# First operands joined in one array of 3 KB rows, and the S5 matrices within a chunk in four column tiles

## The chip, the cores and the metric

The kernel runs on one core of one Trainium2 chip. The metric is the device time of one execution, in microseconds (us). The core has five engines that run side by side, each through its own queue in order: TensorE (PE; its weight loads are shown as PEld), VectorE (DVE), ScalarE (ACT), GpSimd (POOL) and SyncE (SP). SP and POOL issue the DMAs here. Line numbers (L1004) are those of the kernel before.

## The reference

A trunk of four residual layers over 256 tokens of width 1024, in float32. Layer i uses mixer i mod 3: a gated linear recurrence (HGRN2), a matrix memory (mLSTM), a state space (S5), then HGRN2 again. Every layer ends in a SwiGLU FFN with 2816 hidden units:

```
for i in range(4):
    h = mixer[i % 3](x)
    x = layernorm(alpha * x + h)
    x = layernorm(alpha * x + (silu(x @ w_gate) * (x @ w_up)) @ w_down)
```

Two places matter. First, the HGRN2 mixer of layer 0 begins with `q, f, v, g = split(x @ w_in, 4)`. Second, the S5 mixer has 64 groups of 16 channels, each with 64 complex states and a diagonal transition A:

```
state[t] = A * state[t-1] + B u[t]        y[t] = Re(C state[t]) + d * u[t]
```

The kernel cuts the 256 tokens into 64 chunks of four. What a token gives to the outputs of its own chunk is a small matrix per group, with Re(C A^k B) for k = 0 to 3 in its blocks and d on its diagonal. These are the matrices "within a chunk". They depend on the weights alone.

## The kernel before

**Products in three parts.** Each float32 weight or activation is split into a rounded high part, made by an ACT copy (L123 for weights, L1215 for the first x^T), and a low rest, made by a DVE subtraction (L124, L1216). `mm3` then makes a product with three TensorE matmuls: high x high (L140), low x high (L141), high x low (L142). Inside the FFN, `ws_wide` does the same in two matmuls (L170, L173).

**Weights.** `plan` lists all weight tiles in the order of their use, 1 MB each ([128, 2048] floats). `stage_next` takes the next: a DMA on SP's queue (L109) into one of three stage buffers, then the two splits for each half of 1024 columns, into one of eight pairs of split buffers. `wstage` hands out the tile that is due and keeps the staging one tile ahead.

**Start.** `warm_up` runs ten matmuls on zeros (L75). Then `trunk` loads x^T in three pieces, of 2, 2 and 4 row blocks k (L1213), splits each, and stages the first weight tile after the first piece. The first two tiles of layer 0 (w_hg 0 and 1, the two halves over k of the first 512 columns of v) come in three and two pieces (`cuts`, L107). `hgrn` takes them in `block`: `as_part` goes over the two tiles' four halves, in each over the two row halves h of the tokens, and in each of those over two k. The first result is v (L453); then come four gate pairs (`gates`), queries and scores. The POOL queue loads the identity (L50), the head norm weight hnw (L435) and the score masks msk (L439). The identity is read first at L584, msk at L598.

**FFN with S5 preparation beside it.** The FFNs of layers 0 and 1 call `fill` between their parts; it emits some pieces of `s5_prepare`. For each quarter q of the groups these are: `products_b` and `products_bj` (B A^j, on DVE, into the padded tile bz), `products_c` (C A^k for k = 1 to 4 into cu, on DVE, and into the padded cz, on ACT), and then for e = 0, 1: two `turn` (four TensorE transposes each, L987) and one `within`. `within` is called eight times in all.

**`within`.** For each of four group pairs x it makes a block of 32 rows with 64 columns: 16 columns with C itself (L1002, from bc) and 48 with C A^1 to C A^3 (L1004, from cu), each as a sum over the real and the imaginary part. All four land in PSUM partitions 0 to 31, beside one another. One DVE operation masks all of them by the parity pattern par (L1008), the diagonal d is added (L1007, L1010), ACT copies the blocks shifted for the later tokens (L1012), and SP writes the result out (L1013). `temps` gives scratch tiles: two buffers of t0, one of t1.

Each engine's work is put in an order of its own by the framework, which moves instructions where their operands allow it; DMAs on one queue are issued in that order, and a wait of one holds those behind it.

Of the kernel before, what the change touches and what calls it, by code (L numbers as in the profile page):

```python
# [9 lines left out]
F32 = mybir.dt.float32  # L10
# [24 lines left out]
class Trunk:  # L35
    def __init__(self, ctx, tc, aps):
        self.ctx, self.tc, self.nc, self.a = ctx, tc, tc.nc, aps
        mk = lambda name, bufs, **kw: ctx.enter_context(tc.tile_pool(name=name, bufs=bufs, **kw))
        self.const = mk("const", 1)
        self.stage = mk("stage", 3)  # L40
        self.split = mk("split", 8)
        self.xp = mk("xp", 3)
        self.gbp = mk("gbp", 1)
        self.small = mk("small", 4)
        self.ps = mk("ps", 2, space=bass.MemoryType.PSUM)
        self.dram = mk("dram", 1, space=bass.MemoryType.DRAM)
        self.n = 0
        c = self.const
        self.ident = c.tile([P, P], F32, name="ident")
        self.nc.gpsimd.dma_start(self.ident, aps["c_ident"])  # L50
# [17 lines left out]
    def warm_up(self, pool):  # L68


        z = pool.tile([P, 512], BF16, name="warm")
        self.nc.vector.memset(z, 0.0)
        ps = self.bank("t")
        for _ in range(10):
            self.nc.tensor.matmul(ps, z[:, 0:P], z, start=True, stop=True)  # L75


# [20 lines left out]
    def stage_next(self):  # L98

        nc = self.nc  # L100
        name, *at = self.plan[self.staged]
        src = self.a[name]
        for i in at:
            src = src[i]
        st = self.stage.tile([P, 2048], F32, tag="w", name=self.uid("w"))
        w = src.shape[-1]
        cuts = {0: (0, 512, 1024, w), 1: (0, 1024, w)}.get(self.staged, (0, w))  # L107
        for c in zip(cuts, cuts[1:]):
            nc.sync.dma_start(st[:, slice(*c)], src[:, slice(*c)])  # L109
        out = []  # L110
        for i in range(w // 1024):
            part = st[:, i * 1024 : (i + 1) * 1024]
            hi = self.split.tile([P, 1024], F32R, tag="hi", name=self.uid("hi"))
            lo = self.split.tile([P, 1024], F32R, tag="lo", name=self.uid("lo"))
            if name == "w_mo":
                for j in range(2):
                    k = 4 * (at[0] // 2) + 2 * i + j
                    r, c = self.rows[:, k : k + 1], slice(j * 512, (j + 1) * 512)
                    nc.scalar.activation(hi[:, c], part[:, c], AF.Copy, scale=r)
                    nc.vector.scalar_tensor_tensor(lo[:, c], part[:, c], r, hi[:, c].bitcast(F32), ALU.mult, ALU.subtract)  # L120
            else:
                for c in (slice(0, 1024),) if self.staged or i else (slice(0, 512), slice(512, 1024)):
                    nc.scalar.copy(hi[:, c], part[:, c])  # L123
                    nc.vector.tensor_tensor(lo[:, c], part[:, c], hi[:, c].bitcast(F32), ALU.subtract)  # L124
            out.append((hi, lo))
        self.ready[self.plan[self.staged]] = out
        self.staged += 1

    def wstage(self, *key, ahead=AHEAD):

# [300 lines left out]
    def hgrn(self, j, gb, lb=None):  # L431

        nc, tc = self.nc, self.tc
        nw = self.const.tile([P, 1], F32, name=f"hnw{j}")
        nc.gpsimd.dma_start(nw, self.a["hg_nw"][j])  # L435
        with tc.tile_pool(name=self.uid("hg"), bufs=1, reuse_waits="tile") as hp, \
                tc.tile_pool(name=self.uid("hw"), bufs=2, reuse_waits="tile") as wp:
            msk = hp.tile([P, len(MASKED), 256], F32, name=self.uid("msk"))
            nc.gpsimd.dma_start(msk, self.a["c_lvl"])  # L439
            ot = self.transposed(hp)  # L440
            v = hp.tile([P, 2, D], F32, name=self.uid("v"))
            g = hp.tile([P, 2, D], F32, name=self.uid("g"))
# [70 lines left out]
            def gates(pr):  # L513
                pre[pr] = self.hgrn_gates(wp, pr, pair_proj(8 + pr), lb)
# [12 lines left out]
            self.table("natural_log_exp_and_others")  # L527
            for pr in range(4):
                gates(pr)
            self.table("silu_and_others")  # L530
            query(0)
            query(1)
# [273 lines left out]
    def s5_prepare(self):  # L806
# [160 lines left out]

        def products_c(q):
            f = slice(8 * q, 8 * q + 8)
            cu, t1 = temps(2, 4, 8, 16)  # L970
            k["cu"] = cu
            for i in range(2):
                p = lambda r: pw[:, r, 0:4, f][:, :, :, None].broadcast_to([P, 4, 8, 16])
                x = k["bc"][:, 2 + i : 3 + i].broadcast_to([P, 4, 8, 16])
                tt(cu[:, i], x, p(0), ALU.mult)
# [19 lines left out]
        def within(q, e):  # L995
            b = 2 * q + e
            ps = self.bank("t")
            for x in range(4):
                f, o = 4 * e + x, ps[0:32, x * 64 : (x + 1) * 64]
                w = lambda i: k["bz"][:, i, f, 3].rearrange("p g c -> p (g c)")  # L1000
                for i in range(2):
                    nc.tensor.matmul(o[:, 0:16], w(i), k["bc"][:, 2 + i, f], start=i == 0, stop=i == 1)  # L1002
                for i in range(2):
                    nc.tensor.matmul(o[:, 16:64].rearrange("p (k c) -> p k c", k=3), w(i), k["cu"][:, i, 0:3, f], start=i == 0, stop=i == 1)  # L1004
            tm = k["tm"]
            dg = tile_("dg", [32, 4, 32])
            tt(dg, self.ident[0:32, None, 0:32].broadcast_to([32, 4, 32]), dd[:, 4 * b : 4 * b + 4, None].broadcast_to([32, 4, 32]), ALU.mult)  # L1007
            tt(tm[0:32].rearrange("p f (k g c) -> p (f k) g c", g=2, c=16), ps[0:32, 0:256].rearrange("p (n c) -> p n c", c=16)[:, :, None].broadcast_to([32, 16, 2, 16]),  # L1008
               par[:, None].broadcast_to([32, 16, 2, 16]), ALU.mult)
# [193 lines left out]
def trunk(tc, aps, out, layers=range(DEPTH), ffn=True):  # L1203
    with ExitStack() as ctx:
# [2 lines left out]
        layers = list(layers)  # L1207
        t.plan = plan(layers, ffn)
        with tc.tile_pool(name="first", bufs=1, reuse_waits="tile") as fp:
            src = fp.tile([P, KD, S], F32, name="xt")  # L1210
            t.warm_up(fp)
            for k in (slice(0, 2), slice(2, 4), slice(4, KD)):
                nc.sync.dma_start(src[:, k], aps["xt"][:, k])  # L1213
                y, dh, dl = src[:, k], t.xh[:, k], t.xl[:, k]
                nc.scalar.copy(dh, y)  # L1215
                nc.vector.tensor_tensor(dl, y, dh.bitcast(F32), ALU.subtract)  # L1216
                if t.staged == 0:
                    t.stage_next()
        spans = None
        late = ctx.enter_context(ExitStack())  # L1220
        for i in layers:
# [49 lines left out]
def consts():  # L1271
    s, c = np.arange(P)[:, None], np.arange(64)[None, :]
    lvl = []
    for m in MASKED:
# [3 lines left out]
    t = np.arange(P)[None, :]  # L1278
    return {
        "c_ident": np.eye(P, dtype=np.float32),  # L1280
        "c_par": np.repeat(np.eye(2, dtype=np.float32), 16, 0)[:, :, None].repeat(16, 2),
        "c_lvl": np.stack(lvl, 1).astype(np.float32),
        "c_caus": np.where(s > t, np.float32(BIG), np.float32(0.0)),
    }
# [2 lines left out]
def layout(i):  # L1287
# [2 lines left out]
    hg = []  # L1290
    for w in i["hgrn_w_in"]:
        hg.append(np.concatenate([cols_as(w[:, 2 * D : 3 * D]), cols_ws(w[:, 0 : 2 * D]), cols_as(w[:, 3 * D :])]))
    ml = i["mlstm_w_in"][0]
    gw = np.zeros((KD, P, P), np.float32)
    for g in range(2):
# [3 lines left out]
    gc = i["ffn_w_gate_up"].reshape(DEPTH, KD, P, 2, NBLK, 2, P).transpose(0, 4, 5, 2, 3, 1, 6).reshape(DEPTH, NBLK, 2, P, 2048)  # L1299
    out = {  # L1300
        "x": x,
        "xt": np.concatenate([x[:P], x[P:][::-1]]).T.reshape(KD, P, S).transpose(1, 0, 2),
        "ln": np.stack([i["ln_g"], i["ln_b"]], 2).reshape(2 * DEPTH, 2, D),
        "lb": i["hgrn_lb_logits"].reshape(DEPTH, HEADS, P).transpose(2, 0, 1),
        "w_hg": np.stack(hg),
# [37 lines left out]
```

## Time and profile before

| | |
|---|---|
| median of 3 runs | 1296.07 us (1295.36 to 1298.86) |
| the profiled execution | 1296.3 us |
| its span on the core | 1294.4 us |
| PE, PEld busy | 1273.3 us, 1073.3 us |
| DVE, ACT, POOL busy | 964.8 us, 710.5 us, 53.8 us |
| moved by DMA | 251.00 MB, mean 194 GB/s |

The span runs from the first to the last instruction of the core, and times within the trace count from its start. A row of the trace in order of time reads: start in us, length in us, engine, line, operation, what it writes <- what it reads, shape, how many; in brackets the idle time before it and what ended that. Busy times of TensorE overlap, since matmuls are pipelined: a matmul's length is longer than the distance to the next one's start. A float32 matmul that isn't split makes two records; a transpose makes one. In a table of windows the columns after the engines are the granted TensorE clock (1.00 is full), the share of the DMA engines' time, and GB/s.

### The profile page before, as it was taken

Reading aid. Unit: us, or ns where it says so; the run is one execution under the profiler, and the core shown is the slowest. Engines: PE = TensorE matmul, PEld = TensorE weight load, DVE = VectorE, ACT = ScalarE, POOL = GpSimd, SP = SyncE. Lnnn points to the kernel's source line nnn. Section 1 sums busy time; section 2 is a strip of 40 time slices with the busy share of each in tenths; the row PEclk is TensorE's granted clock in tenths of the full one; section 3 lists DMA queues with packets and bytes.
Section 4 is the critical chain, followed back from the end, with each engine's and each line's share of the span. In section 5 each row is a group of like instructions: output and inputs, shape, how many; then the busy total and the mean of one; then the engine's idle time right before and its main releaser. Section 6 shows DMA issues by size and latency. Waiting matters only on the chain.

```text
span 1294.4 us, 18807 instructions
## 1 busy us (share of the span) xinstructions
PE 1273.3 (98%) x7206; PEld 1073.3 (83%) x7206; DVE 964.8 (75%) x1664; ACT 710.5 (55%) x1134; POOL 53.8 (4%) x77
## 2 busy tenths in 40 slices
PE   8999999999999999999999999999999999999997
PEld 6987788888788888888878778888879878888885
DVE  5888789786688699768489887666595896766664
ACT  5755475665457555657442456555459544555550
POOL 0000200000100110000010000000010001000001
PEclk9999999999999999999999999999999999999999
DMA  8832376757374257756558737555555323755540
GB/s 313 298 131 100 126 247 213 253 179 261 123 260 163 98 202 254 241 199 230 193 219 292 269 131 260 195 184 180 190 208 187 134 97 116 265 190 192 181 149 32
DMA packets 46313, 251.00 MB, mean 194 GB/s; under 512 B 5344, under 2 KB 9456, under 8 KB 19856
## 3 DMA queue, kind: packets, MB, share of 16 engines
q1 hardware_dynamic: 45712, 248.08, 54.0%
q0 software_dynamic: 512, 1.73, 0.4%
q8 instruction: 56, 0.92, 0.3%
q14 instruction: 33, 0.27, 0.1%
HBM read 236.16 MB, written 13.63 MB: 193 GB/s over the span
## 4 chain that ended last, share of the span: by engine, by line
PE 89%; DVE 5%; ACT 2%; issue 1%; DMA 1%; POOL 1%; SPq 0%; POOLq 0%; DVEq 0%; ACTq 0%
PE g L170 18%; PE g L173 9%; PE g L140 9%; PE g L141 9%; PE g L142 9%; PE a L141 8%; PE a L140 8%; PE a L142 8%; PE a L594 2%; DVE lo L124 1%; PE t L225 1%; PE t L1090 1%; PE g L1078 1%; DMA xt<-in_xt 1%; PE t L987 1%
## 5 line engine op out<-in xcount | busy, mean ns | idle before, releaser
L124 DVE TENSOR_TENSOR lo<-w,hi 128x1024 fp32r<-128x1024 f32 (+1 forms) x394 | 476.4, 1217 | 139.5 <-ACT hi L123 128.2
L123 ACT CAST hi<-w 128x1024 fp32r<-128x1024 f32 (+1 forms) x394 | 411.1, 1049 | 194.3 <-PE a L141 109.8
L170 PE MATMUL g<-xx,hi 128*128 128x512 f32 x1024 | 358.5, 395 | 0.0
L173 PE MATMUL g<-xx,lo 128*128 128x256 f32 x1024 | 267.4, 281 | 0.0
L170 PEld LDWEIGHTS g<-xx,hi 128*128 128x128 f32 x1024 | 186.7, 188 | 34.4 <-DVE sum L305 0.3
L173 PEld LDWEIGHTS g<-xx,lo 128*128 128x128 f32 x1024 | 192.5, 188 | 10.4
L140 PE MATMUL g<-hi,xx 128*128 128x512 f32 x416 | 169.5, 408 | 4.6 <-ACT xx L244 2.8
L141 PE MATMUL g<-hi,xx 128*128 128x512 f32 x416 | 166.8, 401 | 0.6 <-DVE xx L1216 0.6
L142 PE MATMUL g<-lo,xx 128*128 128x512 f32 x416 | 166.3, 402 | 0.0
L141 PE MATMUL a<-hi,hl 128*128 128x512 f32 x344 | 135.8, 395 | 0.0
L140 PE MATMUL a<-hi,hh 128*128 128x512 f32 x344 | 135.5, 396 | 0.0
L142 PE MATMUL a<-lo,hh 128*128 128x512 f32 x344 | 135.4, 394 | 0.0
L304 ACT COPY sum<-g 128x256 f32<-128x256 f32 x128 | 47.7, 373 | 147.4 <-PE g L170 147.1
L305 DVE TENSOR_TENSOR sum<-g,sum 128x256 f32<-128x256 f32 x128 | 54.2, 424 | 72.9 <-ACT sum L304 72.6
L140 PEld LDWEIGHTS g<-hi,xx 128*128 128x128 f32 x416 | 78.9, 190 | 23.2 <-ACT xx L244 4.6
L142 PEld LDWEIGHTS g<-lo,xx 128*128 128x128 f32 x416 | 78.7, 189 | 17.4 <-DVE lo L124 1.1
L141 PEld LDWEIGHTS g<-hi,xx 128*128 128x128 f32 x416 | 79.1, 190 | 16.1 <-DVE xx L1216 1.0
L141 PEld LDWEIGHTS a<-hi,hl 128*128 128x128 f32 x344 | 64.7, 188 | 14.9 <-DVE hl L294 0.5
L142 PEld LDWEIGHTS a<-lo,hh 128*128 128x128 f32 x344 | 64.7, 188 | 14.8
L140 PEld LDWEIGHTS a<-hi,hh 128*128 128x128 f32 x344 | 64.3, 188 | 13.7 <-ACT hh L293 0.6
L140 PE MATMUL g<-xx,hi 128*128 128x256 f32 x200 | 56.5, 283 | 0.0
L141 PE MATMUL g<-xx,lo 128*128 128x256 f32 x200 | 56.4, 282 | 0.0
(301 smaller groups left out, 1847.8 us busy)
## 6 DMA issues: line engine op xcount, KB each, us to landing
w<-in_w_gu SPq DMA_DIRECT2D x88, 1024.0 KB, 5.0
w<-in_w_dn SPq DMA_DIRECT2D x44, 1024.0 KB, 5.0
w<-in_w_hg SPq DMA_DIRECT2D x30, 1024.0 KB, 5.1
w<-in_w_ml SPq DMA_DIRECT2D x12, 1024.0 KB, 5.1
gb<-in_ln SPq DMA_DIRECT2D x8, 1024.0 KB, 4.8
w<-in_w_ho SPq DMA_DIRECT2D x8, 1024.0 KB, 4.9
w<-in_w_so SPq DMA_DIRECT2D x8, 1024.0 KB, 7.2
ct<-s5ct SPq DMA_DIRECT2D x8, 768.0 KB, 8.4
```

What stands on the lines that cost most here:

```text
L123: nc.scalar.copy(hi[:, c], part[:, c])
L124: nc.vector.tensor_tensor(lo[:, c], part[:, c], hi[:, c].bitcast(F32), ALU.subtract)
L140: mm(ps, lh, rh, start=start, stop=False)
L141: mm(ps, ll, rh, start=False, stop=False)
L142: mm(ps, lh, rl, start=False, stop=stop)
L170: whole = lambda: mm(ps, hi[:, c], self.xx[:, k].rearrange("p i t -> p (i t)"), start=k == 0, stop=k == KD - 1)
L173: mm(ps[:, S:], lo[:, c], self.xh[:, k], start=False, stop=False)
L225: nc.tensor.transpose(pt[:, (k % 4) * P : (k % 4 + 1) * P], z[:, k * P : (k + 1) * P], self.ident)
L304: nc.scalar.copy(t, ps[:, S:])
L305: nc.vector.tensor_tensor(t, ps[:, 0:S], t, ALU.add)
L594: nc.tensor.matmul(pl.rearrange("p (h a t) -> p a h t", h=2, a=2)[:, i], kk[:, i * P : (i + 1) * P], view(q, i * P + m, (256 - m, 2), (2 * ...
L987: nc.tensor.transpose(ps[:, x * P : (x + 1) * P], k["bz"][:, i, 4 * e + x].rearrange("p j g c -> p (j g c)"), self.ident)
```

## The change

- x^T and the first two weight tiles lie in one array `first` of [128, 8, 768]: for each k the 256 values of x^T and the 512 of the weights, 3 KB together. `begin` loads it in six DMAs, of k = 0, 1, 2, 3, (4, 5), (6, 7), and splits x^T and then weights after each. It replaces the loop in `trunk`.
- The warm-up has seven matmuls in place of ten.
- The identity is loaded on SP's queue behind `first`. msk and hnw go to SP's queue too, written after the gates.
- In `within`, group pair x has PSUM partitions 32x to 32x + 31: four column tiles of the array. The loop over the real and imaginary part is the outer one. C itself is copied into cu ahead of C A^1, so that one matmul makes all 64 columns. The masking by par becomes four DVE operations, one for each x, each moving its result to partitions 0 to 31.
- par covers 128 partitions. t0 has one buffer, and cu a tile of its own.

```
-        for _ in range(10):
+        for _ in range(7):
...
+    def pair(self):
+        return [self.split.tile([P, 1024], F32R, tag=t, name=self.uid(t)) for t in ("hi", "lo")]
+
+    def halve(self, x, hi, lo):
+        self.nc.scalar.copy(hi, x)
+        self.nc.vector.tensor_tensor(lo, x, hi.bitcast(F32), ALU.subtract)
+
+    def begin(self, pool):
+
+        src = pool.tile([P, KD, S + 512], F32, name="first")
+        out = [self.pair() for _ in range(4)]
+        for k, n in ((0, 1), (1, 1), (2, 1), (3, 1), (4, 2), (6, 2)):
+            self.nc.sync.dma_start(src[:, k : k + n], self.a["first"][:, k : k + n])
+            self.halve(src[:, k : k + n, 0:S], self.xh[:, k : k + n], self.xl[:, k : k + n])
+            wide = lambda y: (y if n == 2 else y[:, k % 2 * 512 : (k % 2 + 1) * 512]).rearrange("p (k c) -> p k c", k=n)
+            self.halve(src[:, k : k + n, S:], *(wide(y) for y in out[k // 2]))
+        for i in range(2):
+            self.ready[self.plan[i]] = out[2 * i : 2 * i + 2]
+        self.staged = 2
+        self.nc.sync.dma_start(self.ident, self.a["c_ident"])
...
-        nc.gpsimd.dma_start(nw, self.a["hg_nw"][j])
...
-            nc.gpsimd.dma_start(msk, self.a["c_lvl"])
...
             for pr in range(4):
                 gates(pr)
+            nc.sync.dma_start(msk, self.a["c_lvl"])
+            nc.sync.dma_start(nw, self.a["hg_nw"][j])
...
-        par = c.tile([32, 2, 16], F32, name="s5par")
+        par = c.tile([P, 2, 16], F32, name="s5par")
...
-            for tag, bufs in (("t0", 2), ("t1", 1)):
+            for tag, bufs in (("t0", 1), ("t1", 1)):
...
-            cu, t1 = temps(2, 4, 8, 16)
-            k["cu"] = cu
+            k["cu"] = tile_("cu", [P, 2, 5, 8, 16])
+            cu, t1 = k["cu"][:, :, 1:], temps(2, 4, 8, 16)[1]
+            nc.scalar.copy(k["cu"][:, :, 0], k["bc"][:, 2:4])
...
-            for x in range(4):
-                f, o = 4 * e + x, ps[0:32, x * 64 : (x + 1) * 64]
-                w = lambda i: k["bz"][:, i, f, 3].rearrange("p g c -> p (g c)")
-                for i in range(2):
-                    nc.tensor.matmul(o[:, 0:16], w(i), k["bc"][:, 2 + i, f], start=i == 0, stop=i == 1)
-                for i in range(2):
-                    nc.tensor.matmul(o[:, 16:64].rearrange("p (k c) -> p k c", k=3), w(i), k["cu"][:, i, 0:3, f], start=i == 0, stop=i == 1)
+            rows = lambda x: slice(32 * x, 32 * x + 32)
+            for i in range(2):
+                for x in range(4):
+                    f = 4 * e + x
+                    nc.tensor.matmul(ps[rows(x), 0:64].rearrange("p (k c) -> p k c", k=4), k["bz"][:, i, f, 3].rearrange("p g c -> p (g c)"),
+                                     k["cu"][:, i, 0:4, f], start=i == 0, stop=i == 1)
...
-            tt(tm[0:32].rearrange("p f (k g c) -> p (f k) g c", g=2, c=16), ps[0:32, 0:256].rearrange("p (n c) -> p n c", c=16)[:, :, None].broadcast_to([32, 16, 2, 16]),
-               par[:, None].broadcast_to([32, 16, 2, 16]), ALU.mult)
+            for x in range(4):
+                tt(tm[0:32, x].rearrange("p (k g c) -> p k g c", g=2, c=16), ps[rows(x), 0:64].rearrange("p (k c) -> p k c", c=16)[:, :, None].broadcast_to([32, 4, 2, 16]),
+                   par[rows(x), None].broadcast_to([32, 4, 2, 16]), ALU.mult)
...
-            src = fp.tile([P, KD, S], F32, name="xt")
             t.warm_up(fp)
-            for k in (slice(0, 2), slice(2, 4), slice(4, KD)):
-                nc.sync.dma_start(src[:, k], aps["xt"][:, k])
...
+            t.begin(fp)
```

More of the change, by code (lines that the diff above doesn't have):

```diff
@@ L49, in __init__ @@
         self.ident = c.tile([P, P], F32, name="ident")
-        self.nc.gpsimd.dma_start(self.ident, aps["c_ident"])
         self.root = c.tile([P, 8], F32, name="root")
@@ L106, in stage_next @@
         w = src.shape[-1]
-        cuts = {0: (0, 512, 1024, w), 1: (0, 1024, w)}.get(self.staged, (0, w))
-        for c in zip(cuts, cuts[1:]):
-            nc.sync.dma_start(st[:, slice(*c)], src[:, slice(*c)])
+        nc.sync.dma_start(st[:, 0:w], src)
         out = []
@@ L112, in stage_next @@
             part = st[:, i * 1024 : (i + 1) * 1024]
-            hi = self.split.tile([P, 1024], F32R, tag="hi", name=self.uid("hi"))
-            lo = self.split.tile([P, 1024], F32R, tag="lo", name=self.uid("lo"))
+            hi, lo = self.pair()
             if name == "w_mo":
@@ L121, in stage_next @@
             else:
-                for c in (slice(0, 1024),) if self.staged or i else (slice(0, 512), slice(512, 1024)):
-                    nc.scalar.copy(hi[:, c], part[:, c])
-                    nc.vector.tensor_tensor(lo[:, c], part[:, c], hi[:, c].bitcast(F32), ALU.subtract)
+                self.halve(part, hi, lo)
             out.append((hi, lo))
@@ L1209, in trunk @@
         with tc.tile_pool(name="first", bufs=1, reuse_waits="tile") as fp:
-            src = fp.tile([P, KD, S], F32, name="xt")
             t.warm_up(fp)
-            for k in (slice(0, 2), slice(2, 4), slice(4, KD)):
-                nc.sync.dma_start(src[:, k], aps["xt"][:, k])
[L1214 to L1218, printed above, removed]
+            t.begin(fp)
         spans = None
@@ L1280, in consts @@
         "c_ident": np.eye(P, dtype=np.float32),
-        "c_par": np.repeat(np.eye(2, dtype=np.float32), 16, 0)[:, :, None].repeat(16, 2),
+        "c_par": np.tile(np.repeat(np.eye(2, dtype=np.float32), 16, 0), (4, 1))[:, :, None].repeat(16, 2),
         "c_lvl": np.stack(lvl, 1).astype(np.float32),
@@ L1292, in layout @@
         hg.append(np.concatenate([cols_as(w[:, 2 * D : 3 * D]), cols_ws(w[:, 0 : 2 * D]), cols_as(w[:, 3 * D :])]))
+    xt = np.concatenate([x[:P], x[P:][::-1]]).T.reshape(KD, P, S).transpose(1, 0, 2)
     ml = i["mlstm_w_in"][0]
@@ L1301, in layout @@
         "x": x,
-        "xt": np.concatenate([x[:P], x[P:][::-1]]).T.reshape(KD, P, S).transpose(1, 0, 2),
+        "first": np.concatenate([xt, hg[0][0:2].reshape(2, P, 4, 512).transpose(1, 0, 2, 3).reshape(P, KD, 512)], 2),
         "ln": np.stack([i["ln_g"], i["ln_b"]], 2).reshape(2 * DEPTH, 2, D),
```

## Prediction

> **What bounds the kernel now.** I read the page's busy table, then the stretches that hold the two edited places, then single records. The page:
>
> ```profile
> span 1294.4 us, 18807 instructions
> PE 1273.3 (98%) x7206; PEld 1073.3 (83%) x7206; DVE 964.8 (75%) x1664; ACT 710.5 (55%) x1134; POOL 53.8 (4%) x77
> PE 89%; DVE 5%; ACT 2%; issue 1%; DMA 1%; POOL 1%; SPq 0%; POOLq 0%; DVEq 0%; ACTq 0%
> ```
>
> TensorE is busy 98% and makes 89% of the chain that ended last, so time taken off TensorE's own queue should come off the span, if its stretch has no other engine close behind. The two edits sit in two kinds of stretch: the first 22 us, and the two FFNs beside which the S5 matrices are prepared. Of the latter, one ten-microsecond window (columns: PE, PEld, DVE, ACT, POOL busy):
>
> ```profile
> 250.00:260.00 10.00, 10.00 (x80) 8.42 (x80) 5.25 (x7) 5.09 (x9) 0.00 (x0) 1.00 0.72 247
> ```
>
> PE never rests and DVE and ACT are half idle, so there PE alone decides. The first 22 us look different. Instructions in order of time, one engine's start first, then its length:
>
> ```profile
> 1.18 4.45 PE L75 MATMUL t<-warm 128*128 128x512 bf16 x10 [1.18 <-DVE warm L72]
> 4.46 0.62 ACT L1215 CAST xx<-xt 128x512 fp32r<-128x512 f32 x1 [2.46 <-DMA xt<-in_xt]
> 5.12 0.69 DVE L1216 TENSOR_TENSOR xx<-xt,xx 128x512 fp32r<-128x512 f32 x1 [4.00 <-ACT xx L1215]
> 5.83 0.69 PE L140 MATMUL g<-hi,xx 128*128 128x512 f32 x1 [0.20 <-ACT hi L123]
> 10.83 0.73 PE L140 MATMUL g<-hi,xx 128*128 128x512 f32 x2 [1.18 <-ACT xx L1215]
> 12.45 1.05 ACT L123 CAST hi<-w 128x1024 fp32r<-128x1024 f32 x1 [0.23 <-DMA w<-in_w_hg]
> 13.72 1.04 ACT L123 CAST hi<-w 128x1024 fp32r<-128x1024 f32 x1 [0.22 <-DMA w<-in_w_hg]
> 21.73 0.28 PE L140 MATMUL g<-xx,hi 128*128 128x256 f32 x1
> ```
>
> The block that makes the first half of v has 8 k x 2 row halves x 3 = 48 matmuls. It begins at 5.83, and 21.73 is the next block: 15.9 us. The chain shows what one matmul costs there:
>
> ```profile
> 3.06 8.10 DMA xt<-in_xt
> 15.19 0.43 PE g L141
> 18.40 0.23 PE g L140
> ```
>
> At 0.233 us (the 0.23 row; ten steps of them run 18.40 to 20.73) 48 take 11.2 us. So 4.7 us are lost: the third piece of x^T lands at 11.2 and holds the chain, and the matmuls around 15 us run at 0.43. The same stretch by microsecond, the last three columns being granted clock, DMA share and GB/s:
>
> ```profile
> 3.00:4.00 1.00, 1.00 (x4) 0.30 (x3) 0.00 (x0) 0.00 (x0) 0.12 (x1) 1.00 1.00 270
> 9.00:10.00 1.00, 0.65 (x3) 0.19 (x1) 0.00 (x0) 0.79 (x1) 0.00 (x0) 1.00 1.03 334
> 10.00:11.00 1.00, 0.17 (x1) 0.17 (x2) 0.71 (x1) 0.78 (x2) 0.00 (x0) 1.00 0.98 369
> 11.00:12.00 1.00, 0.56 (x2) 0.12 (x2) 1.00 (x2) 0.83 (x1) 0.00 (x0) 1.00 1.05 422
> 14.00:15.00 1.00, 1.00 (x4) 0.72 (x4) 0.96 (x2) 0.76 (x1) 0.31 (x1) 0.50 0.97 410
> ```
>
> PE stands idle around 10 us, and the granted clock is halved after it. While rows of 2 KB load (the first pieces) the queues move 270 GB/s with the engines full; with the rows of 4 KB at 11 us, 422.
>
> **Part 1, the start.** Removed: three x^T pieces and five weight pieces, three warm-up matmuls, and the POOL loads of ident, hnw and msk from this stretch. Added: six loads of 384, 384, 384, 384, 768 and 768 KB, each bringing x^T and weights of the same k, and smaller splits.
>
> Landings, as estimates from the rows above. The first 256 KB landed at 4.46; 128 KB more at 270 GB/s is 0.5: k=0 at 4.95. Rows of 3 KB lie between 270 and 422; I take 330, so 393 kB every 1.2 us: k=1 to 3 at 6.15, 7.35, 8.55. The two 786 kB loads, rows of 6 KB, at 420: 10.4 and 12.3, against 13.72 now.
>
> ```profile
> L304 ACT COPY sum<-g 128x256 f32<-128x256 f32 x128 | 47.7, 373 | 147.4 <-PE g L170 147.1
> L305 DVE TENSOR_TENSOR sum<-g,sum 128x256 f32<-128x256 f32 x128 | 54.2, 424 | 72.9 <-ACT sum L304 72.6
> L124 DVE TENSOR_TENSOR lo<-w,hi 128x1024 fp32r<-128x1024 f32 (+1 forms) x394 | 476.4, 1217 | 139.5 <-ACT hi L123 128.2
> ```
>
> Splitting one k costs ACT 0.37 + 0.62 and DVE 0.42 + 0.69 (128x256 and 128x512; 0.37, 0.42 and 1.22 are these rows, the others are above), and a pair of k ACT 0.62 + 1.05, DVE 0.69 + 1.22.
>
> So the first matmul starts at 4.95 + 0.99 = 5.9, as before. It is what follows that moves. The order is h0 k0, h0 k1, h1 k0, h1 k1 (the loops of as_part): h0 k1 waits for its low half at about 7.8 (6.15 + 0.99 + 0.69), then pairs cost 2.8 us each: to 9.5, then 12.3 (k2, k3); k4 and k5 have their low half at about 13.3 (10.4 + 1.67 + 1.22), one short wait, to 15.6; k6 and k7, ready by 15.2, to 18.4. That is with the full clock. With a half clock until, say, 9.7 (the seven warm-ups end at 1.18 + 7 x 0.43 = 4.2, so PE rests 1.7 us), about 9 matmuls are done by then, later data are all there in time, and 39 x 0.233 ends it at 18.8. I take 18.5 against 21.73: **3.2 us gained**, bounds 1.4 (half clock to 13.1: 17 done, 31 left, end 20.3) and 4.2 (k=0 lands 0.3 us earlier and the 3 KB rows go at 422: end about 17.5).
>
> Does it last to the end? From 22 to 56 PE is continuous in the chain, so the whole program slides. The next weights queue behind 3 MB that land 1.4 us earlier, and msk's 768 KB leave their place ahead of them. On SP's queue are now ident (64 KB, 0.2 us at 420) and, after the gates, msk and hnw. Their first readers:
>
> ```profile
> 57.21 0.69 DVE L584 TENSOR_TENSOR att<-a,ident 128x512 f32<-128x512 f32 x1 [1.44 <-PE a L583]
> 59.89 0.73 DVE L598 COPY_PREDICATED att<-msk,a 128x256 f32<-128x256 int32 x1
> 33.44 7.21 SPq L109 DMA_DIRECT2D w<-in_w_hg  x3
> ```
>
> msk goes between weight loads of about 33 to 45 us and is wanted at 57: cost nothing. If its tile were not free in layer 3, the weight loads behind it on SP's queue would stand; it lay on POOL's queue, with nothing behind it.
>
> **Part 2, the S5 matrices.** One call of `within` (eight in all) on PE, and the records after it:
>
> ```profile
> 252.49 0.30 PE L1002 MATMUL t<-bc,big 128*32 128x16 f32 x4
> 252.63 0.34 PE L1004 MATMUL t<-t,big 128*32 128x48 f32 x4
> 252.81 0.28 PE L1002 MATMUL t<-bc,big 128*32 128x16 f32 x4
> 253.52 0.34 PE L1004 MATMUL t<-t,big 128*32 128x48 f32 x4
> 253.79 0.66 PE L987 MATMUL t<-ident,big 128*128 128x128 f32 x4
> L1004 PE MATMUL t<-t,big x128: 206/206/209, 252.6 to 636.4; 128*32 128x48 f32 x128
> ```
>
> A call runs 252.49 to 253.79, 1.30 us, for 32 records: each f32 matmul is two (128 records of L1004 over 8 calls are 16, for 8 matmuls). Starts are 35 ns apart with 16 columns (four in 0.14) and 45 ns with 48 (four in 0.18). After the change a call has 8 matmuls, 16 records, of 64 columns. No row shows 32 weights with 64 columns; the rows around it are these, the first from the chain (128 columns, whole array), the others from the order of time, where outputs alternate between two 64-wide column tiles:
>
> ```profile
> 56.28 0.89 PE a L583 x8
> 691.47 0.61 PE L1090 MATMUL t<-ct,s5hs 128*64 128x128 f32 x8
> 691.90 0.39 PE L1090 MATMUL t<-ct,s5u 128*64 128x128 f32 x4
> ```
>
> 128 columns cost 111 ns a record alone (0.89 / 8), but 54 where two column tiles alternate (eight from 691.47 to 691.90). So a record of 64 columns alone is 45 + 16/80 x (111 - 45) = 58 ns, and 16 in a row are 0.93 us: the upper bound, no overlap. Overlap in pairs as in L1090 would give 0.46; but no row here has 32-column records closer than 35 ns on average, and 16 of those are 0.56. I take 0.56: 1.30 - 0.56 = 0.74, times 8 = **6.0 us gained**; bounds 3.0 (0.93) and 6.7 (0.46).
>
> What is added beside PE: the masking by par is four DVE operations of 128 columns in place of one of 512, and the copy of the first C block into cu (128x256) is a 0.37 us ACT copy four times, 1.5 us. The prices:
>
> ```profile
> L1008 DVE TENSOR_TENSOR tm<-t,s5par x8: 671/672/672, 254.6 to 637.3; 32x512 f32<-32x512 f32 x8
> L1007 DVE TENSOR_TENSOR dg<-ident,s5dd x8: 273/278/280, 166.2 to 619.3; 32x128 f32<-32x128 f32 x8
> 273.72 0.67 DVE L1008 TENSOR_TENSOR tm<-t,s5par 32x512 f32<-32x512 f32 x1
> 280.93 0.68 DVE L975 TENSOR_TENSOR t<-bc,s5pw 128x512 f32<-128x512 f32 x1
> ```
>
> 4 x 0.28 - 0.67 = 0.45, times 8 = 3.6 us of DVE. It hides under PE, as the 250 to 260 window shows (DVE 5.25 of 10); without that cover 3.6 + 1.5 would be the price. The copy on ACT waits for the old cu's readers, the last `within` of the quarter before; queued behind it are the casts that the next FFN matmuls need. That `within` is over before 273.72 and the next quarter's C products start at 280.93, so it waits for nothing. One t0 buffer in place of two: its writers and nearly all its readers are DVE in order; nothing.
>
> **Sum.** -3.2 - 6.0 = -9.2 us. The profiled execution took 1296.3 us (span 1294.4), the median of the runs is 1296.07; from the median, **1286.9**. A measurement of this kernel can tell about 0.3%, 3.9 us, from no change.
>
> The Trainium skill's page "TensorE: Matmul & The Clock Gate", Part 1 ("The HAM clock gate"), says that the array is at half clock by default and gets the full one after a busy window of about 3.4 us, counted free of the kernel's start. Seven warm-ups take 3.0 us and would by that rule not fill a window, so it speaks against this edit, and the sum would be rival A's. The half clock after the pause at 10 us fits the rule; no run here has seven.
>
> **The rivals.** *A, the clock stays low.* PE rests between 4.2 and 5.9, and is granted half speed until 13.1 or a little later. For it: the half clock after the idle time at 10 us. Against: the slow matmuls themselves keep PE busy. The block then ends at 20.3, gain 1.4: 1288.7.
>
> *B, the column tiles do not overlap.* 0.93 us a call, gain 3.0: 1289.9. For it: both records of one matmul go to one tile. Against: L1090, also two records a matmul, overlaps.
>
> *C, slower: changing the column tile empties the array.* Place: the eight tile changes in each call. Just ahead of the call shown above the array goes from 128 columns to 32:
>
> ```profile
> 252.16 0.40 PE L142 MATMUL a<-lo,hh 128*128 128x512 f32 x1
> ```
>
> The next start should be at 252.39 and is 0.10 later. A call would cost 0.93 + 8s; with the 3.2 of the start the kernel is slower than before from s = (1.30 + 0.40 - 0.93) / 8 = 0.10 on. With s = 0.15 (that 0.10 and half as much for the first record, which runs longer): 8 x (0.93 + 1.2 - 1.30) - 3.2 = +3.4, 1299.5. Against: L1090 changes tiles at once.
>
> *D, the gains are lost on the way.* A new order of DVE and ACT work, or msk on SP's queue, gives back some 6 of the 9 us (the uncovered 5.1 and a load's wait): 1293.
>
> *E, all four tiles run at once.* L1090 halves the time with two tiles; four could quarter it: 16 x 58 / 4 = 0.23 us a call, gain 8.6 and 11.8 in all: 1284.3. Against: the floor of 35 ns. The skill's same page, Part 3 ("Measured speedup vs the span model"), has such tiles start about 4 ns apart and finish in little more than one matmul's time; L1090's pairs bear that out for two tiles, no run here for four.
>
> **Chances.** Forecast 0.54, A 0.14, B 0.12, E 0.07, C 0.05, D 0.08. The range takes in A and B and the bounds of the forecast: low 1284.8 (4.2 + 6.7 = 10.9, and a little), high 1291.9 (A and B together: -1.4 - 3.0 = 1291.7). C, D and E, 0.20, lie outside. Faster by over 0.3% needs 1292.2 or less: forecast, A, B and E hold 0.87, less 0.03 for part of their gain lost as in D: 0.84. Within 0.3%: D, that 0.03 and 0.01 of C, 0.12. Slower: the rest of C, with s a little over 0.15, 0.04.
>
> **What would show it.** Right: the first block's end (first 128x256 matmul) at 18 to 19 us; no granted clock of 0.50 between 13 and 16; `within` spans of 0.5 to 0.6 us with half the records; PE still 10.00 in the windows beside them; DVE busy up by about 3.6 us. Wrong: matmuls at 0.43 past 10 us (A), record starts 58 ns apart (B), gaps at each tile change (C), PE waiting for lo, cu or tm (D). The forecast fails if the block ends after 20.3 or a call takes over 0.93.

## The result, and the profile after

The changed kernel takes 1285.67 us in the median (1284.4 to 1287.76, four runs), against 1296.43 for the kernel before (four runs): 10.8 us less, a ratio of 0.992 with a 95% interval of 0.9907 to 0.9932. The forecast was 1286.9 in a range of 1284.8 to 1291.9.

The page of the changed kernel, where the span is 11.8 us shorter than before:

```profile
span 1282.6 us, 18578 instructions
PE 1262.3 (98%) x7075; PEld 1064.1 (83%) x7075; DVE 968.5 (76%) x1692; ACT 711.1 (55%) x1142; POOL 51.1 (4%) x72
PE 89%; DVE 5%; ACT 2%; issue 1%; POOL 1%; DMA 1%; SPq 0%; POOLq 0%; DVEq 0%; ACTq 0%
```

PE is busy 11.0 us less, has the same 98% of the span, and the same 89% of the chain. DVE has 3.7 us more, and DVE's share of the chain stays at 5%. The first 18 us in order of time:

```profile
1.18 3.01 PE L74 MATMUL t<-warm 128*128 128x512 bf16 x7 [1.18 <-DVE warm L71]
4.46 0.40 ACT L127 CAST xx<-first 128x256 fp32r<-128x256 f32 x1 [2.45 <-DMA first<-in_first]
5.43 0.50 PE L155 MATMUL g<-hi,xx 128*128 128x512 f32 x1 [1.25 <-ACT hi L127]
8.36 0.41 ACT L127 CAST xx<-first 128x256 fp32r<-128x256 f32 x1 [1.08 <-DMA first<-in_first]
10.25 0.62 ACT L127 CAST xx<-first 128x512 fp32r<-128x512 f32 x1 [0.96 <-DMA first<-in_first]
11.87 0.50 PE L155 MATMUL g<-hi,xx 128*128 128x512 f32 x1 [0.36 <-ACT hi L127]
12.15 0.62 ACT L127 CAST xx<-first 128x512 fp32r<-128x512 f32 x1 [0.33 <-DMA first<-in_first]
17.87 0.28 PE L155 MATMUL g<-xx,hi 128*128 128x256 f32 x1
```

ACT rows that waited for a DMA give the landings: k=0 at 4.46, k=3 at 8.36, the pairs at 10.25 and 12.15. The block starts at 5.43 and the next one at 17.87 instead of 21.73: 3.86 us. Of its 12.44 us, 11.2 are work. By microsecond (the last three columns are granted clock, DMA share, GB/s):

```profile
3.00:4.00 1.00, 1.00 (x4) 0.16 (x2) 0.00 (x0) 0.00 (x0) 0.00 (x0) 1.00 0.90 323
6.00:7.00 1.00, 1.00 (x6) 0.82 (x5) 1.00 (x4) 0.98 (x3) 0.00 (x0) 1.00 0.99 396
10.00:11.00 1.00, 1.00 (x6) 0.80 (x5) 0.12 (x2) 0.75 (x2) 0.00 (x0) 1.00 1.07 420
14.00:15.00 1.00, 1.00 (x6) 0.82 (x5) 0.98 (x1) 0.17 (x1) 0.00 (x0) 1.00 1.01 426
```

PE works through the microsecond from 10 to 11, in which it was busy for 0.17 before, and the clock is 1.00 at 14 us where it was 0.50. One `within`, and the records around it:

```profile
248.22 0.40 PE L157 MATMUL a<-lo,hh 128*128 128x512 f32 x1
248.55 0.26 PE L1018 MATMUL t<-cu,big 128*32 128x64 f32 x4
248.55 0.43 PE L1018 MATMUL t<-cu,big 128*32 128x64 f32 x16
248.91 0.66 PE L1003 MATMUL t<-ident,big 128*128 128x128 f32 x4
L1018 PE MATMUL t<-cu,big x128: 219/219/243, 248.5 to 624.8; 128*32 128x64 f32 x128
L1024 DVE TENSOR_TENSOR tm<-t,s5par x32: 278/284/292, 249.0 to 626.0; 32x128 f32<-32x128 f32 x32
L987 ACT COPY cu<-bc x4: 403/407/408, 160.2 to 575.1; 128x256 f32<-128x256 f32 x4
```

The first of the two L1018 rows shows only the stretch up to 248.575: by then four records have started, within 0.03 us. The whole call takes 0.36 us to the next record, where it took 1.30. Eight times 0.94 is 7.5 us. With the start's 3.9 that is 11.4 of the span's 11.8. The first call of `within` starts 3.9 us earlier than before (248.55 against 252.49), the eighth 10.6 (624.63 against 635.21), and it ends 11.5 earlier (624.99 against 636.52): the gain grows call by call, as it should if nothing between is lost.

So both gains exist. Which part of each edit makes them was then tried with twelve kernels. Differences are against runs of the kernel before beside each.

| run | median us | before | ratio, 95% interval | second block starts, us | one `within`, us |
|---|---|---|---|---|---|
| s5_only | 1288.6 | 1295.76 | 0.9942, 0.9928 to 0.9955 | 21.47 | 0.36 |
| start_only | 1292.8 | 1295.76 | 0.9978, 0.9969 to 0.9987 | 17.25 | 1.30 |
| one_tile | 1290.22 | 1295.76 | 0.9958, 0.9944 to 0.9971 | 18.26 | 1.01 |
| two_tiles | 1287.86 | 1296.9 | 0.9933, 0.9919 to 0.9948 | 18.96 | 0.57 |
| x_outer | 1284.87 | 1295.76 | 0.9916, 0.9903 to 0.993 | 18.46 | 0.38 |
| pool_back | 1285.43 | 1294.85 | 0.9924, 0.9909 to 0.9938 | 18.49 | |
| rows15 | 1285.02 | 1294.85 | 0.9922, 0.9904 to 0.994 | 18.18 | |
| warm0 | 1285.49 | 1294.85 | 0.9924, 0.9909 to 0.9938 | 18.44 | |
| order_only | 1294.24 | 1296.9 | 0.9986, 0.9977 to 0.9995 | 18.86 | 1.30 |
| old_order | 1288.18 | 1296.9 | 0.9936, 0.9921 to 0.9951 | 19.58 | |
| singles | 1289.82 | 1294.85 | 0.9957, 0.9942 to 0.9972 | 20.76 | |
| singles_ahead | 1286.84 | 1296.9 | 0.9926, 0.991 to 0.9943 | 19.31 | |

Where the text below speaks of the first block's end, it means this start of the second, except in singles, where a wait lies between. The start of start_only, one_tile, two_tiles and x_outer is the changed kernel's, and yet their blocks end at 17.25, 18.26, 18.96 and 18.46, against its 17.87. So a difference of a few tenths of a microsecond between two profiles' blocks says nothing about an edit.

### The profile page after: what moved, and what is told of

Read it like the earlier page. It is cut to its first block, busy times and chain, and to the rows that moved or that the text cites. A ratio compares the mean times of both kernels' runs of the same rounds, so it can differ in the third digit from the quotient of the medians.

```text
span 1282.6 us, 18578 instructions
## 1 busy us (share of the span) xinstructions
PE 1262.3 (98%) x7075; PEld 1064.1 (83%) x7075; DVE 968.5 (76%) x1692; ACT 711.1 (55%) x1142; POOL 51.1 (4%) x72
## 4 chain that ended last, share of the span: by engine, by line
PE 89%; DVE 5%; ACT 2%; issue 1%; POOL 1%; DMA 1%; SPq 0%; POOLq 0%; DVEq 0%; ACTq 0%
PE g L185 18%; PE g L188 9%; PE g L155 9%; PE g L157 9%; PE g L156 9%; PE a L156 8%; PE a L155 8%; PE a L157 8%; PE a L609 2%; DVE lo L128 1%; PE t L240 1%; PE t L1106 1%; PE g L1094 1%; DMA first<-in_first 1%; PE t L1003 1%
## 5 line engine op out<-in xcount | busy, mean ns | idle before, releaser
L128 DVE TENSOR_TENSOR lo<-w,hi 128x1024 fp32r<-128x1024 f32 x389 | 472.4, 1221 | 121.5 <-ACT hi L127 113.1
L127 ACT CAST hi<-w 128x1024 fp32r<-128x1024 f32 x389 | 406.7, 1051 | 192.3 <-PE a L156 110.9
L188 PEld LDWEIGHTS g<-xx,lo 128*128 128x128 f32 x1024 | 192.4, 188 | 10.4
L156 PEld LDWEIGHTS a<-hi,hl 128*128 128x128 f32 x344 | 64.8, 188 | 14.8 <-DVE hl L309 0.3
L157 PEld LDWEIGHTS a<-lo,hh 128*128 128x128 f32 x344 | 64.7, 188 | 14.8
```

What stands on the lines that cost most here:

```text
L127: self.nc.scalar.copy(hi, x)
L128: self.nc.vector.tensor_tensor(lo, x, hi.bitcast(F32), ALU.subtract)
L156: mm(ps, ll, rh, start=False, stop=False)
L157: mm(ps, lh, rl, start=False, stop=stop)
L188: mm(ps[:, S:], lo[:, c], self.xh[:, k], start=False, stop=False)
```

## The experiments

### The two parts, each alone

**s5_only** is the kernel before with the edits to `within`, cu, par and t0, the lines of the diff from par on without the last ones, on `src` and `begin`.

> The S5 part alone, with the start as before. Theory (the two gains are separate and both on TensorE's own queue): each of the eight calls of within takes 0.36 us to the next record in place of 1.305, 7.6 us off the span, nothing at the start: about 1288.8. Rival (part of what the S5 part shows was the start's, through a shifted order of the work): less than 6 us gained, and the distance between the calls differs from 0.94 each.

**start_only** is the changed kernel with just those edits taken back.

> The start alone, with the S5 matrices as before. Theory: the first block ends near 17.9 in place of 21.7, 3.9 us gained (3 to 4.5 with where the clock's change falls), all of it kept to the end: about 1292.4. Rival (the start's gain in one profiled execution was an accident of where the clock dropped): 1 to 2 us.

The medians fall by 7.2 and 3.0 us, 10.1 together, against 10.8 for both; the 3.0 lie between start_only's theory (3.9) and its rival (1 to 2). In the profiles a `within` takes 0.36 us in the one, and the first block ends at 17.25 in the other. The parts add up within the intervals, and the S5 part is the larger.

### What in `within` makes the gain

**one_tile**: 64 columns at once, but all four group pairs in partitions 0 to 31, side by side, with the one masking operation of before; the loop over x is the outer one.

```
-                    nc.tensor.matmul(ps[rows(x), 0:64].rearrange(...
+                    nc.tensor.matmul(ps[0:32, 64 * x : 64 * x + 64].rearrange(...
```

> The changed kernel with one matmul of 64 columns for each group pair and part, but all four group pairs in PSUM partitions 0 to 31, one column tile, and one masking operation. Theory (the column tiles run side by side and that is most of the S5 gain): 16 records about 57 ns apart, a call 0.85 + 0.15 = 1.0 us to the next record, 5 us slower than the changed kernel. Rival (fewer and wider matmuls make the gain, tiles add little): a call of 0.4 to 0.6 us, less than 2 us slower.

**two_tiles**: group pairs 0 and 1 in two column tiles, then 2 and 3 in the same two, in the next 64 columns.

```
-            rows = lambda x: slice(32 * x, 32 * x + 32)
-            for i in range(2):
-                for x in range(4):
+            rows = lambda x: slice(32 * (x % 2), 32 * (x % 2) + 32)
+            for y in range(2):
+                for i in range(2):
+                    for x in (2 * y, 2 * y + 1):
...
```

> The changed kernel with two column tiles in place of four: group pairs 0 and 1 side by side, then 2 and 3, in two column ranges of PSUM. Theory (every tile runs down its own list, one record of 64 columns each 56 ns): eight steps of 56 ns, a call of 0.45 + 0.02 + 0.13 = 0.58 to 0.62 us to the next record, 2 us slower than the changed kernel. Rival (the gain of tiles is not in proportion): 0.4 or 0.9 us.

One call of each in order of time, first one_tile, then two_tiles:

```profile
248.95 1.08 PE L1017 MATMUL t<-cu,big 128*32 128x64 f32 x16
249.96 0.55 PE L1003 MATMUL t<-ident,big 128*128 128x128 f32 x3
```

```profile
249.32 0.64 PE L1019 MATMUL t<-cu,big 128*32 128x64 f32 x16
249.89 0.55 PE L1003 MATMUL t<-ident,big 128*128 128x128 f32 x3
```

1.01, 0.57 and 0.36 us for the same 16 records in one, two and four tiles. Halving the steps takes off 0.44 and then half of that, 0.21: 16, 8 and 4 steps of 0.055 us, and a part of about 0.14 that stays. Most of that part lies at the end: in all three traces 0.15 us pass from the start of the call's last record to the next record, where a step takes 0.056. Perhaps that is the way out of the narrow shape; no run tries it. Wider matmuls alone give 0.29 of the 0.94 us (1.30 to 1.01), the tiles 0.65. In time one_tile is 5.5 us faster than the kernel before where the changed kernel is 10.8.

**x_outer**: the two loops exchanged, so that two matmuls of one tile follow each other.

```
-            for i in range(2):
-                for x in range(4):
+            for x in range(4):
+                for i in range(2):
```

> The changed kernel with the loops exchanged: for each group pair the real part and then the imaginary part, so two matmuls in a row go to the same column tile. Theory (matmuls start in the order of the program; one waits for its own tile and holds those behind it): the tiles overlap only where the next tile follows, about 5 steps of 114 ns: a call of 0.57 + 0.1 = 0.65 to 0.75 us, 2.5 to 3 us slower than the changed kernel. Rival (each tile runs down its own list): 0.36 us as before the exchange, no difference.

```profile
249.13 0.45 PE L1018 MATMUL t<-cu,big 128*32 128x64 f32 x16
249.52 0.55 PE L1003 MATMUL t<-ident,big 128*128 128x128 f32 x3
```

0.38 us and no loss of time: the theory of a strict order, which forecast 0.65 to 0.75, fell. A matmul that waits for its own tile did not hold those for other tiles. The framework could have put the old order back, but the starts speak against it: the call's first four starts lie 0.013 us apart here and 0.007 in the changed kernel, as fits two matmuls in place of one before each change of tile.

### What in the start makes the gain

Four kernels each take one thing back or away. **rows15** keeps loads, bytes and order, but the array lies in memory as [16, 128, 384], rows of 1.5 KB:

```
-            self.nc.sync.dma_start(src[:, k : k + n], self.a["first"][:, k : k + n])
+            self.nc.sync.dma_start(src[:, k : k + n].rearrange("p k (r c) -> p (k r) c", r=2), self.a["first"][2 * k : 2 * (k + n)].rearrange("r p c -> p r c"))
```

> The changed kernel with the same six loads of the same bytes in the same order, but from an array in which each row of 3 KB lies in two pieces of 1.5 KB. Theory (the row size sets the rate): GB/s between 4 and 10 us fall to 250 to 300, the landings of k = 3 and of the last load come 2 us or more later, the block ends at 20 or later, some 2 us slower. Rival (the order of the loads matters, not the row): rate near 400, block ends near 17.9.

**pool_back** issues ident, hnw and msk from POOL's queue at their old places.

```
+        self.nc.gpsimd.dma_start(self.ident, aps["c_ident"])
...
+        nc.gpsimd.dma_start(nw, self.a["hg_nw"][j])
...
+            nc.gpsimd.dma_start(msk, self.a["c_lvl"])
```

> The changed kernel with the loads of ident, hnw and msk back on POOL's queue at their old places. Theory (joined rows of 3 KB made the loads fast, the POOL loads were small beside them): GB/s between 4 and 10 us stay above 370, the first block ends within 0.4 us of 17.9. Rival (taking the POOL loads out of this stretch made the gain): under 330 GB/s there, the block ends 1 us or more later.

**warm0** has no warm-up matmuls.

```
-            t.warm_up(fp)
```

> The changed kernel without the seven warm-up matmuls. Theory (the clock rises only after some microseconds of work, wherever the window falls): the first matmuls run at 0.43 us for 3 to 7 us from 5.4 on; 8 to 16 of the 48 at half clock cost up to 0.2 us each beyond what the waits for data hide: the block ends 0.5 to 3 us later. Rival (the loads set the block's end, the clock does not): ends within 0.4 us of 17.9.

Windows of rows15 (two), pool_back (two) and warm0 (two):

```profile
5.00:6.00 1.00, 1.00 (x2) 0.83 (x3) 1.00 (x2) 0.93 (x2) 0.00 (x0) 1.00 0.88 253
7.00:8.00 1.00, 1.00 (x4) 0.81 (x3) 0.30 (x1) 0.74 (x2) 0.00 (x0) 1.00 1.01 356
```

```profile
6.00:7.00 1.00, 1.00 (x4) 0.81 (x3) 0.99 (x3) 0.35 (x2) 0.00 (x0) 1.00 1.02 218
7.00:8.00 1.00, 1.00 (x3) 0.77 (x3) 0.55 (x2) 0.84 (x2) 0.00 (x0) 1.00 0.81 240
```

```profile
8.00:9.00 1.00, 1.00 (x4) 0.81 (x3) 0.64 (x2) 0.93 (x2) 0.00 (x0) 1.00 1.03 412
10.00:11.00 1.00, 1.00 (x6) 0.79 (x6) 0.42 (x1) 1.00 (x2) 0.00 (x0) 1.00 1.02 414
```

The rates do sag: to 253 and 356 GB/s with the short rows, to 218 and 240 while the POOL loads run, against 381 to 421 in the changed kernel. The blocks still end at 18.18, 18.49 and 18.44, and the medians lie 9.4 to 9.8 us under the kernel before. Neither the long rows, nor the freed queue, nor the warm-up makes the gain by itself. All three profiles show three or four matmuls a microsecond, 0.43 us apart, until about 9.4 us and then six (warm0's pair of rows), and still lose only 0.3 to 0.6 us at the block's end: while TensorE is slow the data run ahead of it. The clock column reads 1.00 in all these windows, since the trace's clock record begins only with the rise, at 9.3 to 9.5 us here; before it the distance of the matmuls tells the clock. By what was expected, pool_back's theory (over 370 GB/s) and rows15's (20 us or later) missed, and neither rival held in full. warm0's 0.6 us is within its theory (0.5 to 3), but pool_back, with seven warm-ups, is as late.

What was left is the order of the bytes. **order_only** is the kernel before, with its arrays, POOL loads and ten warm-ups; only the first loads and splits go in the order of k, x^T of two k and then the weights of the same two (so the last x^T piece, of four k, becomes two):

```
-            for k in (slice(0, 2), slice(2, 4), slice(4, KD)):
+            for q in range(4):
+                k = slice(2 * q, 2 * q + 2)
                 nc.sync.dma_start(src[:, k], aps["xt"][:, k])
...
+                for c in (slice(0, 1024),) if q else (slice(0, 512), slice(512, 1024)):
+                    part = st[:, o + c.start : o + c.stop]
+                    nc.sync.dma_start(part, aps["w_hg"][0][q // 2][:, o + c.start : o + c.stop])
```

> The kernel before, with its arrays, its ten warm-ups and its POOL loads kept, but the first loads and splits in the order of k: x^T of two k, then the weights of the same two, four times (rows of 2 and 4 KB). Theory (the order of the bytes makes the start's gain; rows, POOL loads and warm-ups do not): the first block ends between 17.9 and 19 in place of 21.7, some 3 us faster than the kernel before. Rival (it takes the joined array): the block ends after 20.5, under 1.2 us gained.

**old_order** is the changed kernel with `first` loaded and split in the old order. Each load now takes a part of the array's rows, so that the pieces are 1 and 2 KB long:

```
-        for k, n in ((0, 1), (1, 1), (2, 1), (3, 1), (4, 2), (6, 2)):
+        for part, new, hi, lo in (x(0, 2), w(0, 1), w(1, 1), w(2, 2), x(2, 2), x(4, 4), w(4, 2), w(6, 2)):
```

> The changed kernel, but its array first is loaded and split in the old order: x^T of k = 0, 1, then the weights of k = 0 to 3, then the other x^T, then the other weights. No POOL loads, seven warm-ups. Theory (the order): x^T of k = 2, 3 lands after 8 us, TensorE waits some 2 us and more for it, the block ends at 20 to 21.7, 2 to 4 us slower than the changed kernel. Rival (the order does not matter, the six steps and the queue do): the block ends by 18.5.

The end of the block in order_only; then old_order's waits and end, in order of time:

```profile
18.86 0.39 PE L140 MATMUL g<-xx,hi 128*128 128x256 f32 x1
```

```profile
10.24 0.73 PE L159 MATMUL g<-hi,xx 128*128 128x512 f32 x2 [0.55 <-ACT xx L127]
11.58 0.50 PE L160 MATMUL g<-hi,xx 128*128 128x512 f32 x1 [0.61 <-DVE xx L128]
19.58 0.28 PE L159 MATMUL g<-xx,hi 128*128 128x256 f32 x1
```

Order alone takes the old kernel's block from 21.73 to 18.86, 2.9 of the 3.9 us, with rows of 2 and 4 KB and everything else as it was. About half of that has the size of the low clock: in the kernel before, nine matmuls from 12.97 to 16.61 took 3.6 us in place of 2.1. Such a fall in the first block stands in both profiles with the old start (before and s5_only), and in none of the twelve others, order_only among them. Of the 2.9 us, 2.2 are left in the span (1292.2 against 1294.4). The timed gain is 0.14% (0.05 to 0.23), about 1.8 us; the medians lie 2.7 apart.

Undoing the order costs the changed kernel 1.7 us and brings back the waits for x^T of k = 2, 3 at 10.2 and 11.6. That is less than the 2 to 4 us expected: here the clock did not fall after the waits, as it did at 13 us in the kernel before. Nor is all of the 1.7 the order's: with the shorter pieces the queues moved 232 to 368 GB/s from 5 to 9 us, and by 10 us 2.5 MB had come in place of 2.9. Even with the old order the block ends 2.2 us before that of the old kernel. So order is the largest single part of the start's gain that a run shows, and not all of it.

### Smaller loads still

**singles** loads each k by itself, to take away the waits at 11.9 and 13.1 for the split of the pair (4, 5).

```
-        for k, n in ((0, 1), (1, 1), (2, 1), (3, 1), (4, 2), (6, 2)):
+        for k, n in [(k, 1) for k in range(KD)]:
```

> The changed kernel with eight loads of one k each in place of six. Theory (the waits at 11.3 to 11.9 and 12.9 to 13.1 come from the two double loads' long splits): k = 4 is split by about 10.5, those waits go, the block ends 0.4 to 0.8 us earlier. Rival (smaller loads and more splits cost as much on SP's and ACT's queues): ends within 0.2 us, or later.

The waits inside the block are gone, but its clock rose only at 10.4, and its last matmul starts at 18.74, against 17.64 in the changed kernel; 0.4 to 0.8 us earlier were expected. By the medians it is some 4 us slower than the changed kernel. ACT, and the last and first matmuls of the two blocks, in order of time:

```profile
18.74 0.40 PE L157 MATMUL g<-lo,xx 128*128 128x512 f32 x1
19.17 0.60 ACT L466 ACTIVATE v<-g 128x512 f32<-128x512 f32 x1 [0.80 <-PE g L157]
19.67 2.93 ACT L127 CAST hi<-w 128x1024 fp32r<-128x1024 f32 x3
20.76 0.38 PE L155 MATMUL g<-xx,hi 128*128 128x256 f32 x1 [1.62 <-ACT hi L127]
```

The framework had moved ACT's splits of the next weight tile behind the copies of v, which wait for the block's end. In the changed kernel they ran at 14.8, beside it. **singles_ahead** adds one line, which writes these splits ahead of the block:

```
         self.staged = 2
+        self.stage_next()
```

> Eight loads of one k each, as in the run with single loads, with the splits of the next weight tile (the first gate pair's) written ahead of the first block, so that ACT makes them before the copies of v. Theory (the single loads lost time because ACT made those splits after the copies of v, and TensorE waited 2.5 us; the block itself had no waits): no wait at the second block, 3 us or more faster than with single loads, level with the changed kernel or up to 1 us ahead where the clock rises as early. Rival (the lost time came from the clock's window or from the loads): within 1.5 us of the run with single loads.

It is 10.1 us faster than the kernel before, where singles is 5.0. The profiles show 3.0 us between the two spans: the second block starts 1.45 earlier (19.31 against 20.76), and most of the rest lies near 700 us, where the clock was low in singles and not in singles_ahead (last section). So the place of two casts on ACT's queue is worth about 1.5 us by the trace; what makes up the rest of the timed difference is open. Two waits of 0.2 and 0.9 us are left at the second block, so the expectation of none failed. Its median is 1.2 us above the changed kernel's, with intervals that overlap. No kernel tried beats the changed one by more than the intervals.

## Why the prediction held, point by point

- **TensorE decides, so what leaves its queue leaves the span.** Right: 11.0 us less PE, 11.8 us less span, the share of the chain unchanged.
- **The start, 3.2 us.** 3.9 in the profile, 3.0 in the median of start_only. The forecast block end of 18.5 lies within the 17.25 to 18.96 that profiles with this start show. Landings forecast for k=0, k=3 and the pairs: 4.95, 8.55, 10.4, 12.3; found: 4.46, 8.36, 10.25, 12.15. In place of one short wait for the split of (4, 5) there are two, for its high part to 11.87 and for its low part to 13.13. The first matmul came 0.5 us earlier than forecast.
- **The reason given for it was partly wrong.** "Rows of 3 KB lie between 270 and 422; I take 330": the rate was 323 at 3 us and 381 to 421 from 5 us on, and rows15 shows that 1.5 KB would have done. What counts most is that x^T and weights of one k arrive together (order_only). The working had this only in its walk through the k, not as a cause. It took the third piece of x^T, landed at 11.2, for what held the old block. TensorE waited for the second, of k = 2 and 3: for its high part to 10.83 and for its low part to 12.17, which DVE made behind a split of weights. In the kernel before:

```profile
10.29 1.22 DVE L124 TENSOR_TENSOR lo<-w,hi 128x1024 fp32r<-128x1024 f32 x1 [2.35 <-ACT hi L123]
11.43 2.04 DVE L1216 TENSOR_TENSOR xx<-xt,xx 128x512 fp32r<-128x512 f32 x2
12.17 0.50 PE L141 MATMUL g<-hi,xx 128*128 128x512 f32 x1 [0.61 <-DVE xx L1216]
```

  The rest of the 3.9 us, 1.0 by order_only and 2.2 by old_order, is not assigned to one edit by a run.
- **The S5 matrices, 6.0 us: the term that was mis-sized.** 7.5. The step that failed is "no row here has 32-column records closer than 35 ns on average, and 16 of those are 0.56". Those rows come from one column tile. Between tiles there is no such floor: four records of the changed kernel start within 0.03 us, and a call is four steps of about 56 ns (forecast for a record of 64 columns: 58) and a fixed 0.14 us. The term's own bound, 6.7 us, did not hold it. Rival E had the mechanism, at a chance of 0.07, and overstated it by 1.1 us, since it left out the fixed part.
- **The number.** The two bounds together gave 10.9 us. The span fell by 11.8, the median by 10.8, so the median came in just within them. That is in part luck, as the runs of one kernel spread over some 3 us. Two of the signs named for a right forecast were missed on the early side: a block's end at 18 to 19 us, and a call of 0.5 to 0.6.
- **Cover for the added work.** Right: DVE 3.7 us more (forecast 3.6), four ACT copies of 0.41 us (0.37), and the windows beside it, of the changed kernel, still show PE at 10.00:

```profile
250.00:260.00 10.00, 10.00 (x61) 8.75 (x60) 6.55 (x12) 6.69 (x14) 0.00 (x0) 1.00 0.57 201
```

- **SP's queue.** Right: ident, msk and hnw cost nothing; pool_back gains nothing by moving them back.
- **Rival A, the low clock.** It did not happen in this profile. That was luck: in seven of the ten profiles with seven warm-ups the matmuls are 0.43 us apart until 8.5 to 10.6 us. Four of the seven keep the six loads in their order (one_tile, pool_back, rows15, two_tiles). Their blocks end at 18.26, 18.49, 18.18 and 18.96, against 17.25 to 18.46 in the three profiles whose clock was full, so the low clock cost some 1 us at most, about what the walk with a half clock said (18.8). The Trainium skill's page "TensorE: Matmul & The Clock Gate", Part 1, says that the window is not tied to the kernel's start and that the number of slow matmuls differs from run to run; the profiles agree, with none after the warm-up in the changed kernel and nine in rows15. By the budget of 3.4 us that this page of the Trainium skill gives, seven warm-ups could be too few, and in the seven profiles they were; that it would cost more than 1.8 us, as rival A had it, no profile bore out.
- **Rivals B and C** fell with 0.36 us a call: tiles overlap, and changing tile costs nothing that shows. **D** fell with the ladder of the eight calls.

## What to carry to other kernels

Where the first product of a kernel waits for its loads, put the bytes in the order in which the loop uses them, both operands of one step together; here that was worth more than row length, queues or warm-up. Where many small products with few weight columns share the array, give each a column tile of its own: here the time went down with the number of tiles, and the order of the loops hardly mattered. After such an edit look at what the scheduler did to the other engines' queues: two casts behind the wrong copy cost 1.5 us, more than the 0.4 to 0.8 expected of smaller loads.

## What the runs showed of the hardware that was not expected

The clock can fall late in the kernel too. In the S5 mixer TensorE has pauses, and in the profiles of s5_only, x_outer, singles and old_order the granted clock was 0.50 for 3.4 us near 700 us; in the other ten, the changed kernel's among them, it was not. Two windows of the same work, first s5_only, then the changed kernel:

```profile
700.00:704.00 4.00, 4.00 (x40) 3.72 (x37) 3.93 (x8) 0.09 (x1) 0.00 (x0) 0.57 0.95 378
```

```profile
696.00:700.00 4.00, 4.00 (x55) 3.78 (x56) 3.93 (x9) 1.00 (x2) 0.00 (x0) 1.00 1.03 410
```

40 matmul records in place of 55 in four microseconds. The cost is seen in the first and last start of the same 128 records, in x_outer and then in the changed kernel:

```profile
L1106 PE MATMUL t<-ct,s5hs x128: 272/273/421, 680.6 to 730.4; 128*64 128x128 f32 x128
L1106 PE MATMUL t<-ct,s5hs x128: 272/273/323, 679.9 to 728.1; 128*64 128x128 f32 x128
```

49.8 us against 48.2, so the low clock costs 1.6 us; the four profiles have 49.7 to 49.9 and the other ten 48.1 to 48.2. Both kernels wait 1.3 us for DVE just there, so the wait alone does not decide it. Executions of x_outer fit it, with spans of 1282.9 to 1283.1 us at a mean clock of 0.999 and 1285.0 at 0.997; those of order_only do not all, with 1293.7 at 0.998 as well as at 0.997. That the late fall is what spreads the times of one kernel over 3 us was not tried.
